# A hybrid mLSTM and gated-delta block: the order of weight splits and solve steps, the chunks of the solve, its store, and one projection quantum

## The chip, the cores and the metric

The kernel runs on one core of a Trainium2 chip, as one program from start to end. The metric is the device time of that program in microseconds (us), the median of several runs.

## The reference

One layer of a bidirectional encoder block on 256 tokens of width 2048, in float32. A modulated RMSNorm gives `h`; one wide projection of `h` feeds two branches, a chunkwise mLSTM with 4 heads and a gated delta rule with 16 heads; their merged output is projected and added to `x`, and a SwiGLU block with 5632 hidden columns and a last norm follow. The change lies in the gated delta branch, where each head, chunk of 64 tokens and direction needs the inverse of a unit triangular matrix. Cut to that:

```python
h = rms_norm(x, norm_mix_w) * (1 + scale_m) + shift_m
proj = h @ w_in          # q, k, v and gates of both branches, output gates, merge gates
...
a_mat = eye(64) + beta[..., :, None] * einsum('nbhid,nbhjd->nbhij', kc, kc) * decay_strict
t_mat = triangular_solve(a_mat, eye(64), left_side=True, lower=True, unit_diagonal=True)
u = t_mat @ (beta[..., None] * vc)
w = t_mat @ ((beta * exp(gc))[..., None] * kc)
# then a scan over the chunks with u, w, the decays and a state of 128x128 per head
...
x = x + gate_m * ((g_a * y_a + g_b * y_b) @ w_out)
hf = rms_norm(x, norm_ffn_w) * (1 + scale_f) + shift_f
x = x + gate_f * ((silu(gt) * up) @ w_down)      # gt, up = halves of hf @ w_gate_up
```

## The kernel before

**Projections.** A float32 weight is used as two halves, a high one `wh` (a copy by ACT, the scalar engine) and a low one `wl` (what is left, a subtraction by DVE, the vector engine). Each product on PE (the matrix engine) is then the sum of three matmuls: high by high, high weights by the low half of the activations (`hl`), low weights by their high half (`hh`). Two generators issue this work in quanta. `fjob` makes 128 columns with the weights standing: a quantum is half a block, 24 matmuls of 256 columns. `tjob` makes 512 columns with the tokens standing: a quantum is two of a chunk's four rows of blocks, 12 matmuls of 512 columns. Each quantum needs one split, 128x1024 elements on ACT and the same on DVE. Raw weights come in transfers of 1 MB into three buffers; a new one is issued when the DVE split has freed the old one. `pump`, at the end of each quantum, asks for rows of the modulation weights (`ada`) and from time to time lets DVE multiply one of them (L123).

**Names.** `z` is the gated delta branch's output gate, `ma` and `mb` the merge gates, `o` the mLSTM's output gate, `a` and `b` the projections of the heads of the two branches. `wl_z_2_0` is the split of rows 0 and 1 of chunk 2 of `z`, `wl_b_0_8` the second half of a block of `b`; in the trace the numbers are left out.

**The four groups.** The 16 heads of the delta rule go in groups of four. For a group:
- `gdn_phase1` (one run per head) builds the 32x32 blocks on the diagonal of the triangular matrices in `mi`, and stores them to DRAM (`inst_d`) with POOL's queue; the same queue loads them back as 16 partitions of `uu` per head (L668). Each of the 64 partitions of `uu` then holds one 32x32 block.
- `gdn_invert` inverts these 64 blocks in 30 steps on DVE, each a product into `utmp` (L701) and a sum into `uu` (L707). A step `i` works on `i * (31 - i)` elements of each partition: 30, 58, 84, up to 240 in the middle, and back down to 30. The generator yields between chunks of steps, and `invert` puts one quantum of the projections (`fill(1)`) behind each chunk. Rows 16 to 31 are stored once they are done, the other rows at the end, by four transfers each (L693).
- `gdn_blocks` loads the stored inverses as `cg` (four transfers, L720), transposes them on DVE (L722) and spreads them into `R`, `X` and `UL`, from which the blocks of 64 and then 128 rows are put together.
- `gdn_phase2`, one run per pair of heads, does this (its first solve step: four matmuls, then `pt` on DVE at L759, then four matmuls on `pt`) and the scan. Between its steps the loop takes quanta of the projections of the next group's heads from `stream`; `after` and `second` say how many behind each step of pair 0 and pair 1.

**What sets the order.** The program is written as one stream, and a scheduler may move an instruction ahead of others on its engine when it comes to be ready earlier by its own estimate. `order(...)` keeps an instruction in the place where it is written, relative to the others that are kept. In `gdn_invert` the memset and all steps are kept; the splits of `fjob` and of most of `tjob` are not, so that they go where the scheduler puts them between the steps. The chunks of the solve end when a count of `i * (31 - i) + 125` goes over 580.

Of the kernel before, what the change touches and what calls it, by code (L numbers as in the profile page):

```python
# [25 lines left out]
GRP = 4  # L26
# [26 lines left out]
def hybrid_block(ctx: ExitStack, tc: tile.TileContext, xr, nfr, crow, pk_d, cst_d, ada2, ada4, win0, winb, wint, wba, wbb, wo, wgu, wd, out, dbg=None):  # L53
# [92 lines left out]
    owed, held = [0], [False]  # L146

# [21 lines left out]
    def fjob(name, src, done):  # L169
# [5 lines left out]
        for k0 in range(0, KB, 8):  # L175
            wh = st.tile([P, 8, P], F32R, tag="wh", bufs=3, name=f"wh_{name}_{k0}")
            wl = st.tile([P, 8, P], F32R, tag="wl", bufs=3, name=f"wl_{name}_{k0}")
            S.activation(wh, raw[:, k0 : k0 + 8], AF.Copy)
            settle()
            V.tensor_tensor(wl, raw[:, k0 : k0 + 8], wh.bitcast(F32), ALU.subtract)  # L180
            for k in range(8):
                kk = k0 + k
                PE.matmul(o, wh[:, k], woven(hh[:, kk]), start=kk == 0, stop=False)  # L183
                PE.matmul(o, wh[:, k], woven(hl[:, kk]), start=False, stop=False)  # L184
                PE.matmul(o, wl[:, k], woven(hh[:, kk]), start=False, stop=kk == KB - 1)  # L185
            pump()
            if k0:
                done(o.rearrange("p (c h) -> p h c", h=2))
            yield True
# [5 lines left out]
    def tjob(name, chunks, xh, xl, done, early=0, by_token=None, steps=1, parts=((0, slice(0, 512)), (1, slice(0, 512)))):  # L195
# [7 lines left out]
        def halves(u, k0):  # L203
# [7 lines left out]
            order(V.tensor_tensor(wl, raws[u][:, k0 : k0 + 2], wh.bitcast(F32), ALU.subtract), early)  # L211
# [78 lines left out]
    inv_d = [tc.dram_tile([32, 4, 16, 32], F32, name=f"inv_d{g}") for g in range(NH_B // GRP)]  # L290
# [293 lines left out]
    def gdn_phase1(h):  # L584
# [82 lines left out]
        order(G.dma_start(uus[g][16 * hl_ : 16 * hl_ + 16], inst))  # L667
# [17 lines left out]
    def gdn_invert(g):  # L685
# [3 lines left out]
        inv = inv_d[g].rearrange("j b (x h) i -> h (b x) j i", h=GRP)  # L689

        def store(rows):
            for e in range(GRP):
                G.dma_start(inv[e, :, rows], uu[16 * e : 16 * e + 16, rows])  # L693
# [3 lines left out]
        size = 0  # L697
        for i in range(30, 0, -1):
# [11 lines left out]
            size += i * w + 125  # L710
            if size > 580:
                size = 0
                yield
        store(slice(0, 16))

    def gdn_blocks(g):

        cg = bk.tile([P, 2, 512], F32, tag="uu", bufs=1, name=f"cg{g}")
        for b in range(4):
            G.dma_start(cg[32 * b : 32 * b + 32, 0], inv_d[g][:, b].rearrange("j x i -> j (x i)"))  # L720
# [300 lines left out]
    def invert(g):  # L1021
        gen = gdn_invert(g)
        next(gen)
        fill(4 if g else 6)
        for _ in gen:
            fill(1)

    invert(0)
    for g in range(4):
        blocks = gdn_blocks(g)  # L1030
        next(blocks)
        fill(7 if g else 8)
# [12 lines left out]
        for p in range(2):  # L1045
            pieces = stream(4 * g + 2 * p + 4)
            for n in range(1, 10):
# [7 lines left out]
                for _ in range(last[n] if g == 3 else second[n] if p else after[n]):  # L1055
# [512 lines left out]
```

## Time and profile before

| | before |
|---|---|
| median of 3 runs | 1960.29 us (1959.03 to 1960.35) |
| the profiled execution, its own time | 1962.84 us |
| its span in the trace | 1961.0 us |
| mean granted clock of PE | 0.994 |
| PE busy | 1926.3 us, 98% |
| PE weight loads (PEld) | 1703.2 us, 87% |
| DVE busy | 1405.7 us, 72% |
| ACT busy | 1028.7 us, 52% |
| POOL busy | 116.9 us, 6% |
| DMA | mean 248 GB/s |

The durations come from one profiled execution. A row of a timeline reads: start in us, duration in us, engine, line of the code, operation, result `<-` operands, partitions x elements, how many instructions the row stands for, and in brackets how long the engine had been idle and what it waited for. PE's matmuls overlap: each is shown from its start to the end of its pipeline, so the distance between starts tells the rate. A row of the waits gives the engine and what it waited for, the sum in us, how often, and the longest. A row of the windows gives the length, then for PE, PEld, DVE, ACT and POOL the busy time and the number of instructions, then the granted clock of PE, the DMA engines' busy share and GB/s. A group's row gives the busy time, the mean in ns of one instruction, and the idle time before it. The inversions of groups 0 to 3 begin at 258, 449, 631 and 810 us of the span.

### The profile page before, as it was taken

What the parts mean: (1) busy time and instruction counts of PE and PEld (TensorE: products, weight loads), DVE (VectorE), ACT (ScalarE), POOL (GpSimd) and SP (SyncE); (2) the same over time, 40 slices, a digit from 0 to 9 for tenths busy, and PEclk for the clock granted to TensorE, in tenths of its full rate; (3) what the DMA queues carried; (4) which work ended last, traced back from release to release, by engine and by line L of the source; (5) the groups of instructions that cost most, each with busy time, mean ns of one, the idle gap of its engine ahead of it and who ended that gap; (6) DMA issues with size and microseconds to landing.
All of it is one profiled execution on the core that took longest, in us unless ns stands there. A gap on an engine that the chain in (4) does not pass through costs nothing.

```text
span 1961.0 us, 27095 instructions
## 1 busy us (share of the span) xinstructions
PE 1926.3 (98%) x10418; PEld 1703.2 (87%) x10418; DVE 1405.7 (72%) x2067; ACT 1028.7 (52%) x1553; POOL 116.9 (6%) x211
## 2 busy tenths in 40 slices
PE   8999999999999999999999999999999999999997
PEld 6888889998999899889787888888888888888886
DVE  6779886898788788866677988665665665555554
ACT  3137656775776588555544444644444444444444
POOL 0001210101011101110100000200000000000000
PEclk9999999999999999999999999999999999999999
DMA  9986677666666667687777998566666665555553
GB/s 400 420 355 223 187 249 252 209 229 217 228 211 212 226 217 232 221 285 254 250 294 266 352 348 325 179 242 247 247 248 239 245 246 193 197 211 209 199 206 138
DMA packets 78962, 485.64 MB, mean 248 GB/s; under 512 B 10585, under 2 KB 15969, under 8 KB 24433
## 3 DMA queue, kind: packets, MB, share of 16 engines
q1 hardware_dynamic: 63216, 450.69, 63.0%
q0 software_dynamic: 8160, 17.88, 4.3%
q10 hardware_dynamic: 7458, 15.36, 2.0%
q8 instruction: 81, 1.33, 0.3%
q14 instruction: 47, 0.39, 0.1%
HBM read 467.07 MB, written 16.82 MB: 247 GB/s over the span
## 4 chain that ended last, share of the span: by engine, by line
PE 83%; DVE 7%; DMA 6%; ACT 2%; issue 2%; POOL 0%; SPq 0%; ACTq 0%; DVEq 0%; POOLq 0%
PE acc_gt L230 4%; PE acc_gt L231 4%; PE acc_gt L232 4%; PE acc_up L232 4%; PE acc_up L231 4%; PE acc_up L230 4%; PE acc_d L232 4%; PE acc_d L231 4%; PE acc_d L230 4%; DMA ra<-ada 3%; PE acc_b L183 3%; PE acc_b L185 3%; PE acc_b L184 3%; PE acc_o L232 3%; PE acc_o L230 3%; PE acc_o L231 2%
## 5 line engine op out<-in xcount | busy, mean ns | idle before, releaser
L211 DVE TENSOR_TENSOR wl_d<-raw_d,wh_d 128x1024 fp32r<-128x1024 f32 x88 | 107.7, 1225 | 105.9 <-ACT wh_d L209 105.9
L211 DVE TENSOR_TENSOR wl_up<-raw_up,wh_up 128x1024 fp32r<-128x1024 f32 x88 | 107.7, 1225 | 100.2 <-ACT wh_up L209 100.1
L211 DVE TENSOR_TENSOR wl_gt<-raw_gt,wh_gt 128x1024 fp32r<-128x1024 f32 x88 | 108.2, 1229 | 80.2 <-ACT wh_gt L209 80.2
L183 PE MATMUL acc_b<-hh,wh_b 128*128 128x256 f32 x576 | 163.2, 283 | 0.0
L185 PE MATMUL acc_b<-hh,wl_b 128*128 128x256 f32 x576 | 160.0, 278 | 0.0
L184 PE MATMUL acc_b<-hl,wh_b 128*128 128x256 f32 x576 | 159.5, 277 | 0.0
L209 ACT ACTIVATE wh_d<-raw_d 128x1024 fp32r<-128x1024 f32 x88 | 92.9, 1056 | 126.4 <-PE acc_d L231 117.6
L209 ACT ACTIVATE wh_gt<-raw_gt 128x1024 fp32r<-128x1024 f32 x88 | 92.9, 1055 | 118.6 <-PE acc_gt L231 71.1
L209 ACT ACTIVATE wh_up<-raw_up 128x1024 fp32r<-128x1024 f32 x88 | 92.8, 1055 | 108.1 <-PE acc_up L231 77.1
L123 DVE SCALAR_TENSOR_TENSOR ada<-ada,crow 128x2048 f32<-128x2048 f32 x64 | 146.1, 2283 | 0.0
L230 PE MATMUL acc_gt<-wh_gt,hfh 128*128 128x512 f32 x352 | 135.9, 386 | 0.0
L231 PE MATMUL acc_gt<-wh_gt,hfl 128*128 128x512 f32 x352 | 135.1, 384 | 0.0
L232 PE MATMUL acc_gt<-wl_gt,hfh 128*128 128x512 f32 x352 | 134.2, 381 | 0.0
L230 PE MATMUL acc_up<-wh_up,hfh 128*128 128x512 f32 x352 | 133.4, 379 | 0.0
L231 PE MATMUL acc_up<-wh_up,hfl 128*128 128x512 f32 x352 | 133.4, 379 | 0.0
L232 PE MATMUL acc_up<-wl_up,hfh 128*128 128x512 f32 x352 | 133.4, 379 | 0.0
L230 PE MATMUL acc_d<-wh_d,ffh 128*128 128x512 f32 x344 | 130.5, 379 | 0.0
L231 PE MATMUL acc_d<-wh_d,ffl 128*128 128x512 f32 x344 | 130.5, 379 | 0.0
L232 PE MATMUL acc_d<-wl_d,ffh 128*128 128x512 f32 x344 | 130.4, 379 | 0.0
L557 PE MATMUL first<-x,raw 128*128 128x256 f32 x512 | 114.5, 382 | 7.5 <-ACT x L551 7.5
L557 PEld LDWEIGHTS first<-x,raw 128*128 128x128 f32 x512 | 96.0, 190 | 26.0 <-ACT x L551 13.5
L183 PEld LDWEIGHTS acc_b<-hh,wh_b 128*128 128x128 f32 x576 | 111.9, 194 | 0.1
(383 smaller groups left out, 5258.0 us busy)
## 6 DMA issues: line engine op xcount, KB each, us to landing
ada<-ada SPq DMA_DIRECT2D x64, 1024.0 KB, 6.2
raw_gt<-wgu SPq DMA_DIRECT2D x44, 1024.0 KB, 5.0
raw_up<-wgu SPq DMA_DIRECT2D x44, 1024.0 KB, 4.9
raw_d<-wd SPq DMA_DIRECT2D x44, 1024.0 KB, 4.9
raw_b<-winb SPq DMA_DIRECT2D x36, 1024.0 KB, 5.3
ra<-ada SPq DMA_DIRECT2D x32, 1025.0 KB, 15.6
raw<-win SPq DMA_DIRECT2D x16, 1024.0 KB, 14.5
raw_z<-wint SPq DMA_DIRECT2D x16, 1024.0 KB, 5.1
```

The lines of the kernel that those rows point to most:

```text
L123: order(V.scalar_tensor_tensor(raw, raw, 1.0, row_c[:, :D], ALU.mult, ALU.mult, accum_out=mod[:, c : c + 1]))
L183: PE.matmul(o, wh[:, k], woven(hh[:, kk]), start=kk == 0, stop=False)
L184: PE.matmul(o, wh[:, k], woven(hl[:, kk]), start=False, stop=False)
L185: PE.matmul(o, wl[:, k], woven(hh[:, kk]), start=False, stop=kk == KB - 1)
L209: order(S.activation(wh, raws[u][:, k0 : k0 + 2], AF.Copy), early)
L211: order(V.tensor_tensor(wl, raws[u][:, k0 : k0 + 2], wh.bitcast(F32), ALU.subtract), early)
L230: order(PE.matmul(ps[t], xh[:, kk, c], woven(wh[:, k]), start=kk == 0, stop=False), early and steps > 1)
L231: PE.matmul(ps[t], xl[:, kk, c], woven(wh[:, k]), start=False, stop=False)
L232: PE.matmul(ps[t], xh[:, kk, c], woven(wl[:, k]), start=False, stop=kk == last)
L557: PE.matmul(first[o], raw[:, o], x[:, b], start=b == 0 and o % 2 == 0, stop=b == KB - 1 and o % 2 == 1)
```

## The change

Five edits go together:

- **Fixed order.** A flag `beside` is set in `invert` for groups 1 to 3, behind the quanta that are issued ahead of the first step. While it is set, the DVE splits of both generators are kept in the written order, between the chunks of steps.
- **Chunks.** For groups 1 to 3 each step counts `i * (31 - i) + 200`, a chunk ends above 765, and what is over is carried to the next. The number of instructions between two quanta is then 6, 6, 4, 4, 4, 2, 4, 4, 4, 4, 2, 4, 6, 4, 2. Group 0 keeps its counts.
- **Store.** `inv_d` has the layout of `uu`, so each half of the inverses is stored by one transfer instead of four. The four heads of a group now alternate over the partitions of `uu`, and the loads of `cg` gather the rows.
- **Quanta ahead of the transpose.** For groups 1 to 3, five quanta instead of seven are issued between the loads of `cg` and their transpose.
- **A quantum ahead.** In group 0, pair 1, one quantum of `stream` is taken before the pair's first solve step, and one fewer behind the eighth.

```diff
@@ -144,6 +144,7 @@
 
     count, every = [0], [0]
     owed, held = [0], [False]
+    beside = [False]
 
     def sums(n=1):
 
@@ -177,7 +178,7 @@
             wl = st.tile([P, 8, P], F32R, tag="wl", bufs=3, name=f"wl_{name}_{k0}")
             S.activation(wh, raw[:, k0 : k0 + 8], AF.Copy)
             settle()
-            V.tensor_tensor(wl, raw[:, k0 : k0 + 8], wh.bitcast(F32), ALU.subtract)
+            order(V.tensor_tensor(wl, raw[:, k0 : k0 + 8], wh.bitcast(F32), ALU.subtract), beside[0])
             for k in range(8):
                 kk = k0 + k
                 PE.matmul(o, wh[:, k], woven(hh[:, kk]), start=kk == 0, stop=False)
@@ -208,7 +209,7 @@
             wl = st.tile([P, 2, 512], F32R, tag="wl", bufs=3, name=f"wl_{name}_{u}_{k0}")
             order(S.activation(wh, raws[u][:, k0 : k0 + 2], AF.Copy), early)
             settle()
-            order(V.tensor_tensor(wl, raws[u][:, k0 : k0 + 2], wh.bitcast(F32), ALU.subtract), early)
+            order(V.tensor_tensor(wl, raws[u][:, k0 : k0 + 2], wh.bitcast(F32), ALU.subtract), early or beside[0])
             return wh, wl
 
         todo = [(u, k0) for u in range(len(chunks)) for k0 in (0, 2)]
@@ -287,7 +288,7 @@
     mb_d = [tc.dram_tile([P, 2, 512], F32, name=f"mb_d{g}") for g in range(4)]
     ob_d = [tc.dram_tile([4, P, T], F32, name=f"ob_d{g}") for g in range(4)]
     inst_d = [tc.dram_tile([64, 32, 32], F32, name=f"inst_d{g}") for g in range(NH_B // GRP)]
-    inv_d = [tc.dram_tile([32, 4, 16, 32], F32, name=f"inv_d{g}") for g in range(NH_B // GRP)]
+    inv_d = [tc.dram_tile([64, 32, 32], F32, name=f"inv_d{g}") for g in range(NH_B // GRP)]
 
     hh = big(bigA, F32R, "hh")
     hl = big(bigA, F32R, "hl")
@@ -664,7 +665,7 @@
         final = hl_ == GRP - 1
         if h + 2 < NH_B and not final:
             decay_load(h + 2)
-        order(G.dma_start(uus[g][16 * hl_ : 16 * hl_ + 16], inst))
+        order(G.dma_start(uus[g][hl_::GRP], inst))
         if h + 2 < NH_B and final:
             decay_load(h + 2)
 
@@ -686,15 +687,13 @@
 
         uu = uus.pop(g)
         tmp = bk.tile([64, 256], F32, tag="utmp", bufs=1, name=f"utmp{g}")
-        inv = inv_d[g].rearrange("j b (x h) i -> h (b x) j i", h=GRP)
 
         def store(rows):
-            for e in range(GRP):
-                G.dma_start(inv[e, :, rows], uu[16 * e : 16 * e + 16, rows])
+            G.dma_start(inv_d[g][:, rows], uu[:, rows])
 
         yield
         order(V.memset(uu.rearrange("p j i -> p (j i)")[:, ::33], 1.0))
-        size = 0
+        size, each, chunk = 0, *((200, 765) if g else (125, 580))
         for i in range(30, 0, -1):
             w = 31 - i
             t3 = tmp[:, 0 : i * w].rearrange("p (j c) -> p j c", j=i)
@@ -707,9 +706,9 @@
             order(V.tensor_tensor(uu[:, 0:i, i + 1 :], uu[:, 0:i, i + 1 :], t3, ALU.add))
             if i == 16:
                 store(slice(16, 32))
-            size += i * w + 125
-            if size > 580:
-                size = 0
+            size += i * w + each
+            if size > chunk:
+                size = size - chunk if g else 0
                 yield
         store(slice(0, 16))
 
@@ -717,7 +716,7 @@
 
         cg = bk.tile([P, 2, 512], F32, tag="uu", bufs=1, name=f"cg{g}")
         for b in range(4):
-            G.dma_start(cg[32 * b : 32 * b + 32, 0], inv_d[g][:, b].rearrange("j x i -> j (x i)"))
+            G.dma_start(cg[32 * b : 32 * b + 32, 0], inv_d[g][16 * b : 16 * b + 16].rearrange("x j i -> j x i"))
         yield
         order(V.transpose(cg[:, 1], cg[:, 0]))
         F_, Bt, Ft, B_ = (cg[:, i // 2, (i % 2) * 256 : (i % 2 + 1) * 256].rearrange("p (m c) -> p m c", m=8) for i in range(4))
@@ -1022,14 +1021,16 @@
         gen = gdn_invert(g)
         next(gen)
         fill(4 if g else 6)
+        beside[0] = g > 0
         for _ in gen:
             fill(1)
+        beside[0] = False
 
     invert(0)
     for g in range(4):
         blocks = gdn_blocks(g)
         next(blocks)
-        fill(7 if g else 8)
+        fill(5 if g else 8)
         next(blocks)
         fill(1)
         pairs = [gdn_phase2(g, p) for p in range(2)]
@@ -1044,6 +1045,9 @@
         every[0] = 1
         for p in range(2):
             pieces = stream(4 * g + 2 * p + 4)
+            ahead = not g and p
+            if ahead:
+                next(pieces)
             for n in range(1, 10):
 
                 held[0] = n < 4
@@ -1052,7 +1056,7 @@
                 next(pairs[p], None)
                 if g == 3 and n == (8, 4)[p]:
                     next(first2[p])
-                for _ in range(last[n] if g == 3 else second[n] if p else after[n]):
+                for _ in range(last[n] if g == 3 else second[n] - (ahead and n == 8) if p else after[n]):
                     next(pieces)
             for _ in pairs[p]:
                 pass
```

What the edits do to the queues shows at two places (the lines of the changed kernel are one off: L700 and L706 are the steps, L212 and L181 the splits). The first is DVE at the start of group 1's inversion, from the last splits ahead of it (`dec` belongs to phase 1 of a later head), before:

```order
L211 TENSOR_TENSOR wl_z_1_2_3914<-raw_z_1_3895,wh_z_1_2_3913 128x1024
L593 SCALAR_TENSOR_TENSOR dec_4783<-al_3592,cst 128x256
L594 SCALAR_TENSOR_TENSOR dec_4783<-al_3592,cst 128x128
L211 TENSOR_TENSOR wl_z_2_0_3941<-raw_z_2_3938,wh_z_2_0_3940 128x1024
L211 TENSOR_TENSOR wl_z_2_2_3963<-raw_z_2_3938,wh_z_2_2_3962 128x1024
L696 MEMSET uu_2865 64x32
L701 TENSOR_TENSOR utmp_3852<-uu_2865 64x30
L707 TENSOR_TENSOR uu_2865<-uu_2865,utmp_3852 64x30
L701 TENSOR_TENSOR utmp_3852<-uu_2865 64x58
L707 TENSOR_TENSOR uu_2865<-uu_2865,utmp_3852 64x29x2
L701 TENSOR_TENSOR utmp_3852<-uu_2865 64x84
L707 TENSOR_TENSOR uu_2865<-uu_2865,utmp_3852 64x28x3
```

and in the changed kernel:

```order
L212 TENSOR_TENSOR wl_z_1_2_3911<-raw_z_1_3892,wh_z_1_2_3910 128x1024
L594 SCALAR_TENSOR_TENSOR dec_4774<-al_3581,cst 128x256
L595 SCALAR_TENSOR_TENSOR dec_4774<-al_3581,cst 128x128
L695 MEMSET uu_2859 64x32
L700 TENSOR_TENSOR utmp_3849<-uu_2859 64x30
L706 TENSOR_TENSOR uu_2859<-uu_2859,utmp_3849 64x30
L700 TENSOR_TENSOR utmp_3849<-uu_2859 64x58
L706 TENSOR_TENSOR uu_2859<-uu_2859,utmp_3849 64x29x2
L700 TENSOR_TENSOR utmp_3849<-uu_2859 64x84
L706 TENSOR_TENSOR uu_2859<-uu_2859,utmp_3849 64x28x3
L212 TENSOR_TENSOR wl_z_2_0_3936<-raw_z_2_3933,wh_z_2_0_3935 128x1024
L700 TENSOR_TENSOR utmp_3849<-uu_2859 64x108
```

The memset and the first six instructions of the solve now stand directly behind `wl_z_1_2` and `dec`, and the splits `wl_z_2_0` and `wl_z_2_2`, which stood ahead of the memset, stand behind the first and the second six.

The same place in the middle of that inversion, near the largest steps, before:

```order
L211 TENSOR_TENSOR wl_mb_3_2_4054<-raw_mb_3_4027,wh_mb_3_2_4053 128x1024
L701 TENSOR_TENSOR utmp_3852<-uu_2865 64x228
L707 TENSOR_TENSOR uu_2865<-uu_2865,utmp_3852 64x19x12
L701 TENSOR_TENSOR utmp_3852<-uu_2865 64x234
L707 TENSOR_TENSOR uu_2865<-uu_2865,utmp_3852 64x18x13
L701 TENSOR_TENSOR utmp_3852<-uu_2865 64x238
L707 TENSOR_TENSOR uu_2865<-uu_2865,utmp_3852 64x17x14
L701 TENSOR_TENSOR utmp_3852<-uu_2865 64x240
L707 TENSOR_TENSOR uu_2865<-uu_2865,utmp_3852 64x16x15
L211 TENSOR_TENSOR wl_o_0_0_4082<-raw_o_0_4079,wh_o_0_0_4081 128x1024
L701 TENSOR_TENSOR utmp_3852<-uu_2865 64x240
L211 TENSOR_TENSOR wl_o_0_2_4102<-raw_o_0_4079,wh_o_0_2_4101 128x1024
```

and in the changed kernel:

```order
L212 TENSOR_TENSOR wl_mb_3_2_4043<-raw_mb_3_4022,wh_mb_3_2_4042 128x1024
L700 TENSOR_TENSOR utmp_3849<-uu_2859 64x238
L706 TENSOR_TENSOR uu_2859<-uu_2859,utmp_3849 64x17x14
L700 TENSOR_TENSOR utmp_3849<-uu_2859 64x240
L706 TENSOR_TENSOR uu_2859<-uu_2859,utmp_3849 64x16x15
L212 TENSOR_TENSOR wl_o_0_0_4072<-raw_o_0_4069,wh_o_0_0_4071 128x1024
L700 TENSOR_TENSOR utmp_3849<-uu_2859 64x240
L706 TENSOR_TENSOR uu_2859<-uu_2859,utmp_3849 64x15x16
L700 TENSOR_TENSOR utmp_3849<-uu_2859 64x238
L706 TENSOR_TENSOR uu_2859<-uu_2859,utmp_3849 64x14x17
L212 TENSOR_TENSOR wl_o_0_2_4092<-raw_o_0_4069,wh_o_0_2_4091 128x1024
```

Eight instructions of the solve stood between two splits, and then one; now four stand between any two.

The second place is DVE at the end of phase 1 of a head in group 0, where pair 1 has its first solve step (`pt_0_1` is that step's product, `Et_1` the second step's transpose), before:

```order
L654 STREAM_TRANSPOSE mi_3093<-mb_3094 128x256
L759 TENSOR_TENSOR pt_0_1_3135<-p_0_1_3134,cst 128x512
L180 TENSOR_TENSOR wl_b_0_0_3145<-raw_b_0_3142,wh_b_0_0_3144 128x1024
L180 TENSOR_TENSOR wl_b_0_8_3179<-raw_b_0_3142,wh_b_0_8_3178 128x1024
L770 STREAM_TRANSPOSE Et_1_3220<-p_0_1_3215 128x128
L180 TENSOR_TENSOR wl_b_1_0_3230<-raw_b_1_3227,wh_b_1_0_3229 128x1024
```

and in the changed kernel:

```order
L655 STREAM_TRANSPOSE mi_3087<-mb_3088 128x256
L181 TENSOR_TENSOR wl_b_0_0_3132<-raw_b_0_3129,wh_b_0_0_3131 128x1024
L123 SCALAR_TENSOR_TENSOR ada_3_3017,mod<-ada_3_3017,crow 128x2048
L758 TENSOR_TENSOR pt_0_1_3167<-p_0_1_3166,cst 128x512
L181 TENSOR_TENSOR wl_b_0_8_3174<-raw_b_0_3129,wh_b_0_8_3173 128x1024
L181 TENSOR_TENSOR wl_b_1_0_3216<-raw_b_1_3213,wh_b_1_0_3215 128x1024
L769 STREAM_TRANSPOSE Et_1_3249<-p_0_1_3244 128x128
L181 TENSOR_TENSOR wl_b_1_8_3256<-raw_b_1_3213,wh_b_1_8_3255 128x1024
```

The first split of the block `b_0` and one `ada` product now stand ahead of `pt_0_1`, and `wl_b_1_0` ahead of `Et_1`.

## The prediction

> **What bounds the kernel now.** The page comes first, then the waits of PE in the stretch that holds the four inversions.
>
> ```profile
> PE 1926.3 (98%) x10418; PEld 1703.2 (87%) x10418; DVE 1405.7 (72%) x2067; ACT 1028.7 (52%) x1553; POOL 116.9 (6%) x211
> PE acc_mb L232 <- DVE wl_mb L211: 2.8, 3, 1.6
> PE acc_o L232 <- DVE wl_o L211: 1.5, 2, 1.1
> PE p L767 <- DVE pt L759: 1.2, 1, 1.2
> PE acc_ma L232 <- DVE wl_ma L211: 1.0, 1, 1.0
> ```
>
> PE is the bound over the whole span. What an edit can win is a wait of PE, and these rows hold nearly all there are between 240 and 880 us: six waits for a low half `wl` written by DVE, one for `pt` of a first solve step. A wait costs 0.16 us more than its idle time, since matmuls are shown 0.38 us long and start 0.216 apart. Five of the six lie inside the inversions of groups 1 to 3 (4.5 + 5 x 0.16 = 5.3 us), one behind the last (0.8 + 0.16). The DVE timeline shows the worst kind, in group 1, with ACT's row for the split that is late:
>
> ```profile
> 460.90 1.06 ACT L209 ACTIVATE wh_o<-raw_o 128x1024 fp32r<-128x1024 f32 x1 [0.78 <-PE acc_mb L231]
> 460.61 0.38 DVE L701 TENSOR_TENSOR utmp<-uu 64x228 f32<-64x228 f32 x1
> 463.94 1.21 DVE L211 TENSOR_TENSOR wl_o<-raw_o,wh_o 128x1024 fp32r<-128x1024 f32 x1
> 465.20 0.48 PE L232 MATMUL acc_o<-wl_o,hh 128*128 128x512 f32 x1 [1.10 <-DVE wl_o L211]
> ```
>
> DVE ran eight steps in a row (460.61 to 463.94) while ACT had the high half of a late split ready near 462; PE stood from then until 465.20. And the start of that inversion, DVE's rows and the PE quantum that meets it, then the same two moments in groups 2 and 3:
>
> ```profile
> 444.03 1.20 DVE L211 TENSOR_TENSOR wl_z<-raw_z,wh_z 128x1024 fp32r<-128x1024 f32 x1
> 446.45 1.23 DVE L211 TENSOR_TENSOR wl_z<-raw_z,wh_z 128x1024 fp32r<-128x1024 f32 x1 [1.22 <-ACT wh_z L209]
> 449.21 0.20 DVE L701 TENSOR_TENSOR utmp<-uu 64x30 f32<-64x30 f32 x1 [1.54 <-DMA uu<-inst_d]
> 447.97 0.38 PE L230 MATMUL acc_z<-wh_z,hh 128*128 128x512 f32 x1
> 450.56 0.38 PE L230 MATMUL acc_z<-wh_z,hh 128*128 128x512 f32 x1
> 630.69 0.19 DVE L701 TENSOR_TENSOR utmp<-uu 64x30 f32<-64x30 f32 x1 [2.17 <-DMA uu<-inst_d]
> 628.81 0.38 PE L230 MATMUL acc_z<-wh_z,hh 128*128 128x512 f32 x1
> 810.33 0.19 DVE L701 TENSOR_TENSOR utmp<-uu 64x30 f32<-64x30 f32 x1 [1.67 <-DMA uu<-inst_d]
> 808.96 0.38 PE L230 MATMUL acc_z<-wh_z,hh 128*128 128x512 f32 x1
> ```
>
> DVE idles 1.5 to 2.2 us for the landing of `uu`, and it idles only then because two splits (z_2_0 and z_2_2, at 444.03 and 446.45) stand ahead of the memset in its queue. PE begins the quantum of z_2_0 at 447.97, 628.81 and 808.96, before the first step in each group.
>
> **The change part by part.** *Fixed order at the start.* In the changed DVE queue the memset stands behind z_1_2, and z_2_0 and z_2_2 behind six steps each. The first step waits for `uu`, so both splits wait too; PE is queued behind them. Step sizes:
>
> ```profile
> L701 DVE TENSOR_TENSOR utmp<-uu 64x58 f32<-64x58 f32 x2 | 0.4, 211 | 0.1
> L701 DVE TENSOR_TENSOR utmp<-uu 64x238 f32<-64x238 f32 x2 | 0.8, 399 | 0.1
> ```
>
> A step follows a step after its duration and 0.035 us (0.25 us in the second step, 0.43 in the longest, those between in proportion to their size); a split starts 0.1 us earlier than a step would, holds DVE 1.135 us and is readable after 1.21. Group 1: first step 449.21, six steps 1.39, split readable at 451.8. PE wants it after four matmuls (two that need no `wl` are drawn ahead now), at 447.97 + 0.86 = 448.83. PE waits 3.0 us. Group 2 starts 1.88 behind PE instead of 1.24, so 3.6; group 3 1.37, so 3.1. Behind it a quantum of PE lasts 2.59 us (447.97 to 450.56). The next six steps (108 to 150 elements) and a split take 2.95: another 0.35. Chunks of four (168 to 228) take 2.5 to 2.8: 0.12, 0.23, 0.10. Then the chunk of two gives 0.7 back and nothing is late any more. Per group 3.8, 4.4, 3.9: 12.2 us in all.
>
> *Even chunks.* The same sum over the queue of before gives waits of 1.2 + 0.7, 1.8 + 0.7 and 1.4, together 5.9 where the trace has 5.3. All of these are gone with chunks of two, four and six steps. Net of both, like for like: 12.2 - 5.9 = **+6.3 us**. The landing decides: in issue-to-landing of `uu` the trace has, for groups 1, 2, 3 and 0,
>
> ```profile
> DMA to landing us min/median/max: 5.2/5.2/5.2
> DMA to landing us min/median/max: 4.7/4.7/4.7
> DMA to landing us min/median/max: 5.3/5.3/5.3
> DMA to landing us min/median/max: 2.8/2.8/2.8
> ```
>
> With 2.8 in all three the waits sum to 5.4 (-0.5 us net); with 0.5 more in each, +7.8. I keep the groups' own landings: POOL's queue ahead of them is the same, only the 16 partitions are now every fourth.
>
> *A quantum ahead.* In group 0, pair 1, with the price of an `ada` product from the page:
>
> ```profile
> L123 DVE SCALAR_TENSOR_TENSOR ada<-ada,crow 128x2048 f32<-128x2048 f32 x64 | 146.1, 2283 | 0.0
> 377.67 0.65 DVE L759 TENSOR_TENSOR pt<-p,cst 128x512 f32<-128x512 f32 x1
> 376.93 0.28 PE L184 MATMUL acc_b<-hl,wh_b 128*128 128x256 f32 x1
> 378.37 1.67 PE L767 MATMUL p<-R,pt 128*128 128x32 f32 x8 [1.17 <-DVE pt L759]
> 375.26:378.68 3.42, 2.25 (x20) 2.05 (x18) 3.42 (x12) 2.69 (x9) 0.64 (x2) 1.00 0.54 202
> 378.68:382.09 3.41, 3.41 (x17) 3.41 (x17) 3.41 (x5) 1.47 (x6) 2.45 (x6) 0.50 0.39 61
> 382.09:385.50 3.41, 3.41 (x18) 3.41 (x17) 1.64 (x4) 1.81 (x5) 0.47 (x1) 0.50 0.94 324
> 644.92:648.33 3.41, 1.81 (x9) 1.46 (x9) 3.38 (x6) 1.30 (x2) 2.26 (x4) 1.00 0.97 331
> 648.33:651.74 3.41, 3.41 (x17) 2.99 (x16) 3.17 (x9) 1.28 (x2) 0.00 (x0) 1.00 0.86 282
> ```
>
> The wait does not go: DVE is inside phase 1 of a head until 377.7, and now the split of the pulled quantum takes the place of `pt`. PE waits from 377.04 to 378.9 (1.8 instead of 1.3 us), but then has a whole projection quantum; behind the split DVE has an `ada` product (2.28 us), and `pt` is wanted only after that quantum. The granted clock (next to last but two in the window rows) is 0.50 in two stretches. In the first PE did eight narrow matmuls and few projections; after the second, full of projections, it came back. Filled from 378.9 on, I let it come back one stretch sooner: 15 projection matmuls by 382.09 at 0.213 us, 0.85 us of narrow ones and 23 at 0.112 by 385.50, so 38 against 26: **-1.2 us**. With both stretches still slow +0.3, with none -2.8.
>
> *One store, small rows in the load.* Eight POOL issues of a group become two, of which three leave the path behind the last step:
>
> ```profile
> 482.70 0.17 DVE L707 TENSOR_TENSOR uu<-uu,utmp 64x30 f32<-64x30 f32 x1
> 483.17 2.23 POOL L693 DMA_DIRECT2D inv_d<-uu  x4 [17.48 <-DVE uu L707]
> 489.33 2.00 POOL L720 DMA_DIRECT2D cg<-inv_d  x4 [3.93 <-DMA inv_d<-uu]
> 496.80 0.71 DVE L722 STREAM_TRANSPOSE cg<-cg 128x512 f32<-128x512 f32 x1 [2.74 <-DMA cg<-inv_d]
> ```
>
> From the last step to the transpose is 13.9 us, 2.7 of it DVE idle; five splits stand between them in both orders (two fills fewer make up for the two splits). 3/4 of 2.23, 1.7 us, go, so DVE waits about 1 us. A wait of 2.7 cost PE 0.3 us here; the 0.8 + 0.16 behind group 3 follows such a wait. Both mostly go: **-1.0 us**, at best -1.3; what the load's rows of 128 bytes cost is a rival.
>
> *Clock in the longer waits.* The wait in 644.92:648.33 left PE 1.81 us busy and the next stretch at 1.00; 375.26:378.68 had more, 2.25, mostly narrow matmuls, and lost half. A wait of 3.0 to 3.6 us can leave nearly none. One slow stretch costs 1.7 us of PE and hides the 0.8 us of small waits behind: 0.9 net. I take one in three groups, **+0.9** (0 to +2.7).
>
> The Trainium skill, page "TensorE: Matmul & The Clock Gate", part 1, says the clock halves after an idle window of some 3.4 us that runs freely. By that rule no wait but a whole window would count, and the sum would be 0.9 less; the stretch 375.26:378.68, busy for 2.25, differs from it.
>
> Sum: 6.3 - 1.2 - 1.0 + 0.9 = **+5.0 us**. Against the profiled execution (1962.84, span 1961.0) that is 1967.8; the median of the runs is 2.55 below it, so 1960.29 + 5.0 = **1965.3 us**. 0.2%, 3.9 us, is about what a measurement of this kernel can tell from no change.
>
> **The rivals.**
> *The block lands early.* Without the two splits and the load of raw weights that the second one releases, `uu` could land like group 0's, at 2.8. For: that row. Against: three rows of 5. The start costs what the chunks bring: -0.5 - 1.2 - 1.0 = -2.7, 1957.6. From 3 us sooner on no start wait is left (0.8 us a group), and with no slow clock at 378: 3.2 - 5.9 - 2.8 - 1.0 = -6.5, 1953.8. This is the faster side; the point is a first step no later than 0.9 us behind PE's quantum for -3.9 in all.
> *The load of small rows lands late.* `cg` now gathers 2048 rows of 128 bytes. Today's stores write such rows and land 4.1 to 5.2 us after issue, the loads of 2048 bytes 3.8 to 5.6, so against. DVE may wait 2.6 us before PE does; if it lands 4 us later in groups 1 to 3, the wait is 5 and PE loses 2.4 x 3 = 7: 1972.
>
> ```profile
> DMA to landing us min/median/max: 4.1/4.7/5.2
> DMA to landing us min/median/max: 3.8/5.2/5.6
> ```
>
> The page "DMA: Bandwidth & Descriptors" of the Trainium skill, "Why small descriptors are slow (HBM only)", gives each packet a fixed cost that small rows feel; by it this rival is the likelier one, and these landings do not show it.
> *The fixed order does nothing*: excluded by the order itself, in which the two splits have moved.
>
> **How the numbers follow.** Forecast 0.54 (1962 to 1969), early block with small gain 0.20, early block with large gain 0.15, late load or two and more slow clocks 0.11. Slower by over 0.2% (above 1964.2): 0.45 of the forecast and the 0.11, 0.56. Faster (below 1956.4): 0.15. Within: 0.29. The range leaves out most of the third case and half of the last: 1956.0 to 1971.0; the forecast's own is 1962 to 1969.
>
> **What would show it.** Right: DVE idle about 5 us before the first step of groups 1 to 3, one wait of PE of about 3 us each there, on `wl_z`, and no waits over 0.4 behind it; a wait of 1.6 to 1.9 near 377 on `wl_b`. Wrong: PE's waits in the inversions summing under 6 us; `uu` landing under 4 us after issue; waits after the transposes over 1 us.

## The result, and the profile after

| | before | changed |
|---|---|---|
| median of 6 runs each | 1960.32 us (1959.03 to 1962.04) | 1969.07 us (1967.04 to 1971.10) |
| ratio to before | | 1.0041, 95% interval 1.0031 to 1.0052 |
| span of the profiled execution | 1961.0 us | 1967.0 us |

The change makes the kernel slower by 8 us (6 to 10 by the interval); 5.0 was forecast: on the right side, within the stated range (1956.0 to 1971.0) and at the upper end of the forecast's own (1962 to 1969).

First the changed kernel's engine row of the page, and PE's waits in the stretch of the four inversions (engine, what it waited for, sum in us, times, longest):

```profile
PE 1929.8 (98%) x10418; PEld 1704.2 (87%) x10418; DVE 1405.6 (71%) x2067; ACT 1028.6 (52%) x1553; POOL 105.6 (5%) x187
PE acc_z L233 <- DVE wl_z L212: 8.1, 3, 3.6
PE acc_b L186 <- DVE wl_b L181: 1.7, 1, 1.7
PE vps L607 <- ACT vf L338: 1.3, 3, 0.8
PE p L791 <- DVE pt L780: 1.0, 1, 1.0
```

The waits on `wl_mb`, `wl_o`, `wl_ma` and `wl_a` are all gone, 5.5 us by their rows. In their place stand three on `wl_z`, one in each group: the starts of the inversions. The timeline of group 1 shows how, DVE first and then PE:

```profile
443.14 0.40 DVE L595 TENSOR_TENSOR_SCAN dec<-al,cst 128x128 f32<-128x128 f32 x1
448.05 0.16 DVE L700 TENSOR_TENSOR utmp<-uu 64x30 f32<-64x30 f32 x1 [4.51 <-issue]
449.41 1.21 DVE L212 TENSOR_TENSOR wl_z<-raw_z,wh_z 128x1024 fp32r<-128x1024 f32 x1
448.05 0.38 PE L232 MATMUL acc_z<-wh_z,hl 128*128 128x512 f32 x1
450.68 0.70 PE L233 MATMUL acc_z<-wl_z,hh 128*128 128x512 f32 x2 [2.25 <-DVE wl_z L212]
```

DVE has nothing it may do from 443.5 to 448.05: the split of z_2_0, whose high half is ready, stands behind six instructions of the solve, and these wait for `uu`, whose last load lands at 447.99 (the row of 448.05 names no releaser, that of 630.81 below does). PE stops 0.2 us after 448.05 and goes on at 450.68. Group 2 has the longest of the three, and a slow clock behind it; the windows are those of group 1, then 2, then 3 (windows: length, then busy time of PE, PEld, DVE, ACT, POOL; the third number from the end is the granted clock):

```profile
630.81 0.19 DVE L700 TENSOR_TENSOR utmp<-uu 64x30 f32<-64x30 f32 x1 [5.78 <-DMA uu<-inst_d]
633.46 0.70 PE L233 MATMUL acc_z<-wl_z,hh 128*128 128x512 f32 x2 [3.55 <-DVE wl_z L212]
446.39:449.81 3.42, 2.03 (x10) 1.44 (x8) 1.59 (x8) 1.06 (x1) 0.00 (x0) 1.00 0.56 144
449.81:453.22 3.41, 2.54 (x12) 2.19 (x12) 3.24 (x8) 0.73 (x1) 0.00 (x0) 1.00 0.02 5
630.68:634.10 3.42, 0.64 (x3) 0.58 (x4) 3.05 (x11) 0.00 (x0) 0.00 (x0) 1.00 0.02 6
634.10:637.51 3.41, 3.41 (x10) 2.69 (x9) 3.20 (x9) 1.06 (x1) 0.00 (x0) 0.50 0.22 26
811.60:815.01 3.41, 1.26 (x6) 0.76 (x4) 2.30 (x8) 1.06 (x1) 0.00 (x0) 1.00 0.40 145
815.01:818.42 3.41, 3.23 (x8) 2.57 (x9) 3.20 (x10) 0.00 (x0) 0.00 (x0) 0.50 0.02 5
```

In group 2 the wait left PE 0.64 us of work in one window, and the next ran at half clock; the same in group 3 (1.26 us). Group 1's wait lies across two windows, leaves 2.03 us in the first, and the clock stays. The landings of `uu`, groups 1 to 3, are within 0.6 us of what they were before (5.2, 4.7, 5.3):

```profile
DMA to landing us min/median/max: 5.0/5.0/5.0
DMA to landing us min/median/max: 5.0/5.0/5.0
DMA to landing us min/median/max: 4.7/4.7/4.7
```

Where the time went is read best by PE's own progress. The table takes the start of the n-th projection matmul in both traces (8604 in each) and gives by how much the changed kernel is later:

| place (time in before) | later by, us | what lies between |
|---|---|---|
| 370 | -0.19 | |
| 440 | -0.57 | pair 1 of group 0 |
| 455, 500 | 2.42, 0.36 | group 1: start; steps and transpose |
| 625 | 0.08 | |
| 640, 655 | 5.59, 2.87 | group 2: start and slow clock; steps |
| 805 | 2.88 | |
| 820, 880 | 7.06, 4.71 | group 3: start and slow clock; steps and transpose |
| 1020, end | 6.29, 6.30 | one slow clock stretch at 961.8, where nothing was changed |

Groups 1 to 3 lose 0.9, 2.8 and 1.8 us. The 1.6 us at 961.8 are a half-clock stretch during narrow matmuls that this execution of before does not have. Of the runs below e2, e3 and e5 have one between 954 and 963 too, e4 and e12 have none; what decides it is not known.

### The profile page after: what moved, and what is told of

Read it like the earlier page. It is cut to its first block, busy times and chain, and to the rows that moved or that the text cites. A ratio compares the mean times of both kernels' runs of the same rounds, so it can differ in the third digit from the quotient of the medians.

```text
span 1967.0 us, 27053 instructions
## 1 busy us (share of the span) xinstructions
PE 1929.8 (98%) x10418; PEld 1704.2 (87%) x10418; DVE 1405.6 (71%) x2067; ACT 1028.6 (52%) x1553; POOL 105.6 (5%) x187
## 4 chain that ended last, share of the span: by engine, by line
PE 86%; DMA 6%; DVE 5%; ACT 3%; issue 1%; POOL 0%; ACTq 0%; SPq 0%; DVEq 0%; POOLq 0%
PE acc_gt L231 4%; PE acc_gt L232 4%; PE acc_gt L233 4%; PE acc_up L231 4%; PE acc_up L232 4%; PE acc_up L233 4%; PE acc_d L231 4%; PE acc_d L233 4%; PE acc_d L232 4%; DMA ra<-ada 3%; PE acc_o L231 3%; PE acc_o L232 3%; PE acc_o L233 3%; PE acc_b L184 2%; PE acc_b L185 2%; PE acc_b L186 2%
## 5 line engine op out<-in xcount | busy, mean ns | idle before, releaser
L212 DVE TENSOR_TENSOR wl_d<-raw_d,wh_d 128x1024 fp32r<-128x1024 f32 x88 | 107.7, 1225 | 105.9 <-ACT wh_d L210 105.9
L212 DVE TENSOR_TENSOR wl_up<-raw_up,wh_up 128x1024 fp32r<-128x1024 f32 x88 | 107.7, 1225 | 100.2 <-ACT wh_up L210 100.1
L212 DVE TENSOR_TENSOR wl_gt<-raw_gt,wh_gt 128x1024 fp32r<-128x1024 f32 x88 | 108.1, 1229 | 80.2 <-ACT wh_gt L210 80.2
L186 PEld LDWEIGHTS acc_b<-hh,wl_b 128*128 128x128 f32 x576 | 110.4, 192 | 2.1 <-DVE wl_b L181 2.1
```

## The experiments

All were timed in five rounds beside the kernel before. "Before" in a diff is the kernel before, "changed" the changed one. "Slow stretch" is a window with a granted clock of 0.50. The traces are of one execution each, the times are medians.

**e1, six quanta ahead of the first step** (changed; the two splits go ahead of the memset again):

```diff
-        fill(4 if g else 6)
+        fill(6)
...
-        fill(5 if g else 8)
+        fill(3 if g else 8)
```

> The changed kernel, but in groups 1 to 3 six quanta instead of four are issued ahead of the first step (and three instead of five ahead of the transpose), so that the splits z_2_0 and z_2_2 stand ahead of the memset again; the order stays fixed and the chunks stay even. Theory (the two splits wait in DVE's queue for the landing of uu, and PE behind them): PE's waits on wl_z of 2.4, 3.7 and 2.5 us and the slow clock behind the last two go, the even chunks keep what they gave back (2.1, 2.7 and 2.4 us in the three groups), about 7 us under before or 1953, up to 2 us more if one split fewer ahead of the transpose is felt. Rival (the loss is in the strided load of uu, the gathered rows or the fixed order as such): waits of 2 to 4 us a group stay and the time is that of the changed kernel, 1966 to 1969.

Measured: 1966.25 us, ratio 1.0029 (1.0017 to 1.0042). Half of the theory holds. No wait on `wl_z` is left, none between the steps either, and no slow stretch at 634 or 815. But the gain of 7 us is not there: the run is 6.5 us above before. PE's waits, and what DVE and PE do at the end of group 1:

```profile
PE p L757 <- DVE R L726: 5.2, 2, 3.0
PE p L766 <- DVE pt L758: 1.8, 1, 1.8
501.39 0.71 DVE L721 STREAM_TRANSPOSE cg<-cg 128x512 f32<-128x512 f32 x1 [6.46 <-DMA cg<-inv_d]
503.15 0.48 DVE L726 SCALAR_TENSOR_TENSOR R<-cg,cst,R 128x256 f32<-128x256 f32 x1
502.91 0.80 PE L757 MATMUL p<-R,cc 128*128 128x32 f32 x4 [2.18 <-DVE R L726]
```

DVE idles 6.5 us for `cg`, and PE waits for `R`, with slow stretches behind. The price that was put at "up to 2 us" is three waits of 2.3, 3.2 and 2.0 us and 17 us of slow stretches, in an execution that took 1971.45 us, 5 above the median: the wait has moved from the start of the inversion to its end.

**e2, fixed order one quantum later** (changed):

```diff
-        beside[0] = g > 0
-        for _ in gen:
+        for n, _ in enumerate(gen):
+            beside[0] = g > 0 and n > 0
             fill(1)
```

> The changed kernel, but the fixed order begins one quantum later: z_2_0 stands ahead of the memset, z_2_2 behind twelve instructions of the solve instead of six and six. Theory: the waits shrink in proportion to the sum, from 2.4, 3.7 and 2.5 us to 1.5, 2.9 and 1.6 on z_2_2 (landing of uu, twelve instructions of 3.16 us, a split, against PE one quantum of 2.59 us later); 3 to 5 us under the changed kernel, according to how many slow clock stretches go with them. Rival (a chunk of twelve is the worse the longer it is): as the changed kernel or up to 3 us above.

Measured: 1968.02 us, ratio 1.0037 (1.0024 to 1.0051), not told apart from the changed kernel. The waits on `wl_z` shrink by 0.5 to 0.6 us each, to 1.8, 3.2 and 2.0 us from the distances of the matmuls, where 0.8 to 0.9 was computed, and new ones stand behind the transposes (`wl_a` in group 1, `wl_mb` in group 3):

```profile
PE acc_z L233 <- DVE wl_z L212: 6.5, 3, 3.1
PE acc_mb L233 <- DVE wl_mb L212: 1.1, 1, 1.1
PE acc_a L186 <- DVE wl_a L181: 0.7, 1, 0.7
```

What the start gives, the end takes: 8.1 against 6.5 + 1.1 + 0.7 = 8.3. The 3 to 5 us that the theory expected were wrong for the same reason as in e1.

**e3, no quantum ahead** (changed):

```diff
-            ahead = not g and p
+            ahead = False
```

> The changed kernel without the quantum ahead of the first solve step in group 0, pair 1. Theory (what it gains at the first step is given back at the next waits on pt and vf, since DVE and ACT are late there): 0.4 us above the changed kernel, 0 to 1.5. Rival (it removes two slow clock stretches for good): 2.5 to 3 us above the changed kernel, with 0.50 granted between 378 and 386.

Measured: 1968.52 us, ratio 1.0041 (1.0028 to 1.0054): the time of the changed kernel, 0.4 us under what the theory had and 2.5 to 3 under the rival. The interval of 5 us excludes neither. The trace tells more. PE waits 1.3 us on `pt` as before, and yet the two slow stretches of before do not come. Its first two windows there:

```profile
375.87:379.28 3.41, 2.23 (x19) 1.94 (x18) 3.41 (x13) 1.95 (x5) 0.37 (x1) 1.00 0.53 203
379.28:382.69 3.41, 3.36 (x28) 3.25 (x29) 3.41 (x4) 2.22 (x9) 2.58 (x6) 1.00 0.31 75
```

In before a window with 2.25 us of PE was followed by 0.50; here one with 2.23 is followed by 1.00; and e1, which keeps the quantum, has a slow stretch there. So neither keeping nor removing the quantum decides the clock at that place.

**e4, the store alone** (before, with the changed kernel's `inv_d` and its `uu` strided over the partitions):

```diff
-            for e in range(GRP):
-                G.dma_start(inv[e, :, rows], uu[16 * e : 16 * e + 16, rows])
+            G.dma_start(inv_d[g][:, rows], uu[:, rows])
...
-            G.dma_start(cg[32 * b : 32 * b + 32, 0], inv_d[g][:, b].rearrange("j x i -> j (x i)"))
+            G.dma_start(cg[32 * b : 32 * b + 32, 0], inv_d[g][16 * b : 16 * b + 16].rearrange("x j i -> j x i"))
```

> The kernel before with the store alone: inv_d in the layout of uu, two stores a group, uu strided over the partitions, cg gathered in rows of 128 bytes. Theory (three POOL issues leave the path): DVE idles about 1 us instead of 2.6 to 3.9 ahead of the transpose, PE's waits of 0.3 and 0.9 behind it go, 1.0 us under before. Rival (small rows land late): DVE idles 4 us or more, 1 to 7 us above before.

Measured: 1958.46 us, ratio 0.9994 (0.9985 to 1.0002): 1 us under before, as expected, but not told from no change. Group 2 shows both theories at work; POOL and DVE:

```profile
665.50 2.63 POOL L718 DMA_DIRECT2D cg<-inv_d  x4 [5.25 <-DMA inv_d<-uu]
674.21 0.71 DVE L720 STREAM_TRANSPOSE cg<-cg 128x512 f32<-128x512 f32 x1 [3.90 <-DMA cg<-inv_d]
```

From the first issue of the loads to the last landing are 8.6 us here, 9.6 in group 3 and 5.9 in group 1.

**e5, the quantum ahead alone** (before, with the changed kernel's `ahead` lines):

> The kernel before with the quantum ahead alone. Theory by the runs so far (the slow clock after 378 comes and goes without it; with it PE waits 1.9 us on wl_b, 1.2 on pt and twice 0.4 on vps, without it 1.3 and 0.2): 2.3 us above before, 1 to 3.5. Rival, as predicted: 1.2 us under before, since PE's clock comes back sooner.

Measured: 1962.54 us, ratio 1.0009 (1.0001 to 1.0018): 1.8 us above before. The prediction's sign for this edit was wrong. The waits of pair 1:

```profile
PE acc_b L185 <- DVE wl_b L180: 1.7, 1, 1.7
PE vps L606 <- ACT vf L337: 1.3, 3, 0.8
PE p L792 <- DVE pt L781: 0.2, 1, 0.2
```

**e6, the fixed order alone** (before, with the lines on `beside`; its own chunks):

> The kernel before with the fixed order alone (its own chunks of 8, 6, 4 ... instructions, four quanta ahead of the first step). Theory: first waits of 2.9, 4.2 and 3.0 us on wl_z in groups 1 to 3, 0.5 at the second split, 1 to 1.5 in small waits behind, 13 to 15 us against 6 of before, and slow clock stretches behind the long waits: 8 to 13 us above before. Rival (the loss of the changed kernel comes from its other parts): within 3 us of before.

Measured: 1970.90 us, ratio 1.0051 (1.0039 to 1.0063), 10 us above before, as the theory has it. The first waits are 3.5, 4.7 and 3.3 us; the small ones behind come to less than 0.8 a group, and each of the three is followed by a slow stretch:

```profile
PE acc_z L233 <- DVE wl_z L212: 11.0, 3, 4.5
```

**e7, even chunks with free splits** (changed, without the lines on `beside` and with `ahead = False`):

> The changed kernel without the fixed order and without the quantum ahead: even chunks, five quanta ahead of the transpose, one store. Theory (free splits go between the steps where the scheduler puts them, 7, 6, 4, 5, 8, 1, 7 instructions apart, and z_2_0 and z_2_2 ahead of the memset): no start wait, waits of 0.6 to 1.8 us in the middle as before; as the store alone, 1 to 2 us under before. Rival (the chunks alone bring their 5 us): 5 to 7 us under before.

Measured: 1964.35 us, ratio 1.0018 (1.0009 to 1.0026): above before, against both. Where the splits are free they stand 7, 6, 4, 5, 8, 1 and 7 instructions apart in DVE's queue whatever the chunks, so the waits in the middle stay. What is left of the edit is two quanta fewer ahead of the transpose, and the small rows of the loads. Both can have a part in group 3: the four loads of `cg` take 10.9 us there from first issue to last landing, the longest of all traces, DVE idles 6.9 us before the transpose, and one wait of PE takes 3.7 us, with 10 us of half clock from 859.6 on:

```profile
PE acc_mb L233 <- DVE wl_mb L212: 5.3, 2, 3.7
```

**e8, six quanta, twelve chunks, five quanta** (changed, `ahead = False`):

```diff
-        fill(4 if g else 6)
+        fill(6)
...
-        size, each, chunk = 0, *((200, 765) if g else (125, 580))
+        size, each, chunk = 0, *((160, 785) if g else (125, 580))
```

> Fixed order and one store, without the quantum ahead, six quanta ahead of the first step, twelve chunks, five quanta ahead of the transpose: both ends are given their cover. Theory: no wait on wl_z at the start, none over 0.5 us on R or pt behind the transpose, small waits of 0 to 1.2 us a group in the inversions (chunks of four of the largest instructions and a split take 2.8 us against PE's 2.59): 4 to 7 us under before, 1953 to 1956. Rival (a fixed order has PE wait at one end whatever the cover): waits of 2 us or more a group, as before or above.

Measured: 1970.78 us, ratio 1.0052 (1.0035 to 1.0069). The rival is right: 10 us above before. The end of group 1 and the clock there:

```profile
494.88 0.71 DVE L721 STREAM_TRANSPOSE cg<-cg 128x512 f32<-128x512 f32 x1 [5.98 <-DMA cg<-inv_d]
497.04 1.22 DVE L181 TENSOR_TENSOR wl_a<-raw_a,wh_a 128x1024 fp32r<-128x1024 f32 x1
498.32 0.58 PE L186 MATMUL acc_a<-hh,wl_a 128*128 128x256 f32 x1 [3.40 <-DVE wl_a L181]
494.40:497.80 3.40, 0.52 (x5) 0.33 (x3) 2.85 (x6) 2.10 (x5) 0.00 (x0) 0.99 0.12 41
497.80:501.20 3.40, 2.88 (x13) 2.89 (x14) 2.73 (x3) 0.62 (x1) 0.00 (x0) 0.51 0.52 152
```

Nothing waits at the start or between the steps, and PE waits 3.4 to 4 us in each group for the split that stands behind `cg` and `R` in DVE's queue. The profiled execution, 1966.38 us, was the shortest of six that reach 1978.24.

**e9, the same with the old store** (before, with the lines on `beside`, `fill(6)` ahead and `fill(5)` behind; its own chunks are the twelve):

> The kernel of the run before (fixed order, six quanta, twelve chunks, five quanta) with the old store: eight stores a group and loads of rows of 2 KB. There PE waited 3.6, 3.4 and 4.0 us behind the inversions, and the loads of cg took 9.6 to 10.2 us from the first issue to the last landing, against 6.9 to 7.5 in the kernel before. Theory (the chain from the landing of uu to the transpose, 47 to 48 us, is longer than PE's quanta up to there once PE does not wait at the start): the chain gets 1.7 us longer by POOL and about 2.5 shorter by the loads, the waits behind the transposes stay over 2 us in each group, 1 to 4 us under that run and still above before. Rival (only the rows of 128 bytes are at fault): waits under 1 us, 4 to 6 us under before.

Measured: 1963.59 us, ratio 1.0011 (1.0001 to 1.0021). Between the two: 2 us above before, where e8 is 10 above. DVE still idles 5.4 us for `cg` in group 1, but in groups 1 and 2 of this order one split more stands ahead of the transpose than in e8, so PE has a quantum more:

```profile
499.64 0.71 DVE L723 STREAM_TRANSPOSE cg<-cg 128x512 f32<-128x512 f32 x1 [5.38 <-DMA cg<-inv_d]
PE acc_mb L233 <- DVE wl_mb L212: 2.7, 2, 2.5
PE p L768 <- DVE pt L760: 2.5, 2, 1.3
PE p L759 <- DVE R L728: 1.1, 1, 1.1
```

Of these, the wait of 2.5 stands behind group 3's transpose, one of 1.3 behind group 2's, that of 1.1 behind group 1's. The place of the transpose in the queue counts beside the store, and the run does not part the two.

**e10 and e11, seven quanta behind the steps** (e8, and the kernel of e9, with `fill(7)`):

> The same kernel with the new store, but seven quanta instead of five between the loads of cg and their transpose. Theory: two quanta more are 5.2 us of cover, more than the 3.4 to 4.0 us that PE waited behind the inversions; with no wait at the start, none between the steps and none at the end, 5 to 7 us under before, less what the quanta taken from later places cost there (0 to 2). Rival (under a fixed order the chain gets longer with every quantum put beside it): waits of 2 us or more in each group, as before or above.

> The kernel before with six quanta ahead of the first step and the fixed order: old store, its own twelve chunks, seven quanta ahead of the transpose. Theory: as with the new store and seven quanta, within 2 us of it, since 5.2 us of cover hide the difference of the stores. Rival (the store decides): 3 us or more beside it.

Measured: 1965.36 us, ratio 1.0022 (1.0011 to 1.0033), and 1965.04 us, 1.0018 (1.0009 to 1.0026). In group 1 of e11 one wait of 1.2 us is left; otherwise the waits at the start, between the steps and at the end are gone in both, as the theory has it, and the stores do not matter. Yet both are slower than before: the quanta that were taken for the cover are missing at the end of group 3, where PE now waits for the scan and the mLSTM, with two slow stretches in e10 and three in e11. By the progress of PE, as in the table above, e10 is 12.6 us ahead of before at 950 and 1.9 behind at 960. Its waits there:

```profile
PE px L837 <- DVE on L864: 3.6, 1, 3.6
PE po L826 <- ACT z L808: 0.7, 1, 0.7
```

**e12, one store, loads in wide rows** (before):

```diff
-        order(G.dma_start(uus[g][16 * hl_ : 16 * hl_ + 16], inst))
+        order(G.dma_start(uus[g][hl_::GRP], inst))
...
-        inv = inv_d[g].rearrange("j b (x h) i -> h (b x) j i", h=GRP)
+        inv = inv_d[g].rearrange("j b y i -> (b y) j i")
...
-            for e in range(GRP):
-                G.dma_start(inv[e, :, rows], uu[16 * e : 16 * e + 16, rows])
+            G.dma_start(inv[:, rows], uu[:, rows])
```

> The kernel before with one store a half that writes rows of 128 bytes into the old layout, so that the loads of cg keep their rows of 2 KB; uu strided over the partitions as in the changed kernel. Theory (three POOL issues of 0.56 us leave the chain, and the loads take 5 to 8 us from the first issue to the last landing as in all runs with the old layout, against 5.6 to 10.9 with rows of 128 bytes): from the last step to the transpose 12 to 12.5 us instead of 13.5 to 15, the waits of 0.3 and 0.9 behind the transposes go, 1.0 to 1.5 us under before. Rival (one store with scattered rows lands later by what the issues save): no difference, 13.5 us or more.

Measured: 1957.49 us, ratio 0.9981 (0.9971 to 0.9991): 3.7 us under before, more than expected, and under the changed kernel. From e4, the other run with one store, the intervals do not part it (0.9971 to 0.9991 and 0.9985 to 1.0002). Group 2, and all that is left of PE's waits on low halves:

```profile
669.74 2.01 POOL L719 DMA_DIRECT2D cg<-inv_d  x4 [5.05 <-DMA inv_d<-uu]
676.56 0.71 DVE L721 STREAM_TRANSPOSE cg<-cg 128x512 f32<-128x512 f32 x1 [2.10 <-DMA cg<-inv_d]
PE acc_mb L232 <- DVE wl_mb L211: 2.0, 2, 1.5
PE acc_o L232 <- DVE wl_o L211: 0.9, 2, 0.5
PE acc_ma L232 <- DVE wl_ma L211: 0.3, 1, 0.3
```

From the last step to the transpose are 12.2, 13.0 and 12.4 us (13.9, 13.5 and 15.1 in before), and no wait stands behind the transposes. The table of progress gives 3.2 us in the inversions and at their ends, with the same slow stretch at 379 as before: the gain lies where the edit is.

## Why the prediction was right, and where it was not

**A chain runs beside PE's quanta.** This is what the prediction did not see, and it explains why e1, e2 and e8 did not gain. From the first step to the transpose of `cg` there are 47.2 to 47.8 us in before, 47.4 to 49.5 in the changed kernel, 49.4 to 50.2 in e8, 48.2 to 49.4 in e10 and 45.1 to 46.7 in e12. The chain begins with the landing of `uu`, and the quanta that PE has to do meanwhile are its only cover. e8 and e10 show it: with no wait at the start or between the steps PE waits 3.4 to 4 us behind the transpose in each group, and two quanta more there take these waits away. Over 2 us of e8's longer chain are its loads, 9.6 to 10.2 us from first issue to last landing against 6.9 to 7.5 in before. In e10's groups 2 and 3 DVE does not idle ahead of the transpose, and there the chain does not bind. In before the waits behind the transposes are 0.3 us in group 1 and 0.9 in group 3:

```profile
500.24 0.38 PE L185 MATMUL acc_a<-hh,wl_a 128*128 128x256 f32 x1 [0.16 <-DVE wl_a L180]
861.03 0.48 PE L232 MATMUL acc_mb<-wl_mb,hh 128*128 128x512 f32 x1 [0.78 <-DVE wl_mb L211]
```

That they are so small because 5.4 us of waits between the steps had made PE late is an inference; no run takes those waits alone away. The changed kernel has the wait at the start (8.1 us of rows), e8 at the end, e10 has it nowhere in the groups and pays in the scan of group 3.

The signs that were named ahead are there: DVE idles 4.5, 5.8 and 5.5 us before the first steps of groups 1 to 3, PE waits once on `wl_z` in each, and 1.7 us on `wl_b` near 378; no wait stands behind the transposes.

Point by point:
- *Fixed order at the start*: mechanism, place and size right. First waits forecast at 3.0, 3.6 and 3.1 us; measured, from the distances of the matmuls, 2.4, 3.7 and 2.5. The small waits behind were put at 0.8 a group. In group 1 PE falls behind by another 0.8 up to 462; in groups 2 and 3 nothing is seen of them beside the slow clock. Sum 9.4 in place of 12.2. e1 shows the cause (with the splits ahead of the memset the waits are gone), and e6 that the fixed order alone makes them.
- *Even chunks*: the waits between the steps went, 5.4 us (4.6 by their rows and 0.16 more for each), as forecast (5.9 by its sum over the queue). That all of it counts as gain was taken for granted. It held here, where PE was late from the start; in e8, without waits at the start or between the steps, it does not hold.
- *The landing*: taken as the groups' own, and it was (5.0, 5.0, 4.7). The rival of an early block is excluded. (Its sum takes 3.2 where 0.8 a group makes 2.4; nothing rests on that now.)
- *A quantum ahead*: forecast -1.2, wrong in sign. The wait came as forecast, 1.7 on `wl_b`. That PE's clock comes back sooner was read from one execution. Of ten traces without the edit five have a slow stretch at 378 (before, e6, e9, e10, e12) and five have none; of four with it, one has. And behind the wait, DVE's `ada` product makes a later `pt` and ACT a later `vf` wait: in the changed kernel 1.9 us on `wl_b`, 1.2 on `pt` and twice 0.4 on `vps`, against 1.3 and 0.2 without it. e5 measures 1.8 us slower (0.2 to 3.5).
- *Store*: forecast -1.0; alone it gave 1 us, within noise. The three issues are won, but the rival had a part: in groups 1 to 3 of all traces the loads take 8.3 us from first issue to last landing with rows of 128 bytes (24 of them, 5.6 to 10.9) and 6.7 us with rows of 2 KB (18, 4.1 to 9.0). The Trainium skill, page "DMA: Bandwidth & Descriptors", "Why small descriptors are slow (HBM only)", says that small rows pay a fixed cost each; these landings agree with it, where before's alone did not show it. The ranges overlap, but in the two pairs of runs that differ in the code only by the store and its layout, e8 with e9 and e10 with e11, the loads of wide rows are the shorter in all six groups, by 0.7 to 4.1 us. e12 keeps the one store and the wide rows, and gains 3.7 us.
- *Clock in the longer waits*: forecast one group in three, +0.9 net of the small waits that a slow stretch hides; it was two, and PE fell behind by 1.7 us in each (3.9 to 5.6 and 5.4 to 7.1 in the terms of the table), 3.4 in all or 1.8 net of twice 0.8. The Trainium skill, page "TensorE: Matmul & The Clock Gate", part 1, asks for a whole idle window; here windows with 0.64 and 1.26 us of PE were followed by half clock, and the measurement decides.

So in this trace the three groups give 0.9 + 2.8 + 1.8 = 5.5 us, where 6.3 - 1.0 + 0.9 = 6.2 was forecast. At the starts PE falls behind by 3.3, 5.5 and 4.2 us, 13.0 together against 12.2 + 0.9 = 13.1, and then makes up 7.5, against 5.9 + 1.0. (A wait costs 0.26 us more than its idle time here, not 0.16: after the wait at 450.68 the next matmul starts at 451.00, 0.32 later instead of 0.216.) That the first sum fits so well is luck: smaller waits and one slow stretch more than forecast make up for each other. The median moved by 8, not by the 6.0 of the two spans, since the profiled execution of before, 1962.84 us, is 2.5 above the median of before and that of the changed kernel, 1969.02, is at its median. The former has 6.8 us of half clock at 378, which half of the traces with that schedule lack. With e5's 1.8 us for pair 1 in place of the -0.4 of these two traces, the groups and the pair make 7.3. How often an unprofiled run has that stretch is not known, but the mean granted clock of the runs is on record: 0.996 over the 88 runs of before beside the experiments, of which 14 have 0.994 or less, as the profiled one has, and 0.992 to 0.995 in the six of the changed kernel. So part of the 8 us goes with slow stretches of the clock; the 0.7 that is left over 7.3 is less than the interval can tell.

## What to carry to other kernels

Where a serial chain (land, solve, store, load) runs beside the bound engine's work, measure the chain from end to end against the work that covers it before counting small waits as gain: a wait removed inside comes back at the end if the chain is the longer, as in e1 and e8. A fixed order should not put a split that is ready behind an instruction that still waits for a transfer. The one edit that won time here shortens the chain itself (e12: fewer issues, and the wide rows on the side that is waited for); which of the two brings the gain is not parted.

## What was not expected of the hardware

- Between 240 and 1000 us of these traces, a wait of PE of over 3 us was followed by a window of half clock in every case (3.2 to 4.7 us, 13 waits), one of 2.3 to 2.7 us in three of six, and one of 1.7 to 2.0 us on a split of 512 columns in none of seven.
- What parts the six is how the wait lies on the windows of 3.41 us that the records of the clock mark out. Where half clock followed, a window was left with 1.26 us of PE (the changed kernel's group 3), 0.89 (e3's group 3) or 1.23 (e1's group 1); where it did not, with 2.03 (the changed kernel's group 1), 1.84 (e3's) or 1.53 (e9's group 3). Over all fourteen traces, from 240 to 1200 us, each of the 16 windows with at most 1.3 us of PE was followed by half clock, and 3 of the 11 with 1.5 to 1.9 us. Each such window of 3.4 us takes up to 1.7 us more.
- At 378, windows with 2.25 and 2.23 us of PE were followed by 0.50 in one execution and 1.00 in another. What decides there stays open; no run was made for it.
